# RMS norm with swish on one core: regrouped transfers, two rows by ScalarE in every third unit, and a small scratch transfer ahead of gamma's

## The chip, the cores and the metric

The kernel runs on one core of one Trainium2 chip. Its time is the device time of one execution in microseconds (us), and what stands for a kernel is the median over its runs. A kernel of this size agrees with itself within a few tenths of a microsecond from run to run.

## The reference

The input `x` has 16 x 1024 rows of 512 float32 numbers. Every row is divided by the root of its mean square, scaled by `gamma`, and passed through swish:

```python
rms = np.sqrt(np.mean(x ** 2, axis=-1, keepdims=True) + eps)
x_norm = x / rms * gamma
return (x_norm * (1.0 / (1.0 + np.exp(-x_norm)))).astype(np.float32)
```

33.5 MB are read and 33.5 MB are written; nothing is used twice, so every byte passes the DMA engines once on its way in and once on its way out.

## The kernel before, in words

The 16384 rows are spread over the 128 partitions, so that each partition has 128 rows of 2 KB. The rows of a partition are cut into eleven tiles of 4, 4, 8, six times 16, 8 and 8 rows (`sizes`, L30). A tile is loaded by one DMA and stored by one DMA, from and to the same place in `xb`, a ring of 96 rows a partition (L31, L70). A tile of 16 rows is a transfer of 4 MB. In each partition a tile is one contiguous piece of HBM (L97 to L99), so a transfer consists of 128 packets, one for each partition, of 8, 16 or 32 KB for tiles of 4, 8 or 16 rows.

Loads are issued by SP (L108 to L118), in order. The first two are moved ahead of the program's opening barrier (`early`, L120 to L131). The tiles that begin at rows 96, 112 and 120 use places in the ring that earlier tiles have left: before their loads SP waits for the stores of tiles 0, 1, 2 and of tile 3 (L110 to L117). All other loads are issued at once.

The computation goes in units of four rows (`cn`, L33), 32 of them. For unit k:

- ScalarE (ACT) waits for the tile's load if the unit is the first of its tile (L157, L158). It sums the squares of the fourth row with an accumulating activation (L159), and squares the first three rows into a PSUM buffer, one of two (L166).
- VectorE (DVE) reduces the three squared rows to three sums (`sums`, L204).
- GpSimd (POOL) adds eps (L141) and raises to the power -0.5 (L148).
- VectorE multiplies the four rows by their factor and by gamma, in place, with four instructions (`norm`, L215).
- ScalarE applies silu to the four rows, in place (`swish`, L178).

The order on each engine is written out by hand. VectorE's is sums(k), norm(k-1) (L223 to L233). ScalarE's is square(k), then the stores whose tile has been finished by swish(k-3), then swish(k-2) (L192 to L199). A store is issued from ScalarE's queue (L183) and waits for the count `ends[t]` of finished swishes. So a tile's store stands in ScalarE's instruction order behind the square of a unit three later, and that square may wait for a load. The last tiles' stores come out as soon as their swish is done, because no squares are left then.

Before the loop ScalarE issues the load of gamma, four copies of 2 KB into four partitions of a zeroed tile (L186 to L189), and loads its activation table (L190). VectorE spreads gamma over the partitions with a shuffle (L228) that stands between sums(0) and sums(1), and waits for gamma's landing.

At its end SP waits for the stores (L236 to L238).

Of the kernel before, what the change touches and what calls it, by code (L numbers as in the profile page):

```python
# [8 lines left out]
@with_exitstack  # L9
def kernel(  # L10
    ctx: ExitStack,
    tc: tile.TileContext,
    x: bass.AP,
    gamma: bass.AP,
    eps: bass.AP,
    out: bass.AP,
):
    nc = tc.nc
    P = nc.NUM_PARTITIONS
    AF = mybir.ActivationFunctionType  # L20
    ALU = mybir.AluOpType
    fp32 = mybir.dt.float32
    bf16 = mybir.dt.bfloat16

    xf = x.flatten_outer_dims()
    of = out.flatten_outer_dims()
    R, D = xf.shape


    sizes = [4, 4, 8] + [16] * 6 + [8, 8]  # L30
    ring = 96  # L31
    early = 2
    cn = 4  # L33
    n_sq = 3
    N = sum(sizes)
    assert N * P == R, (N, R)


    tiles = []
    done = 0  # L40
    for sz in sizes:
        assert done % ring + sz <= ring
        tiles.append((done * P, sz, done % ring))
        done += sz
    T = len(tiles)

    chunks = [
        (t, r, r == at)
        for t, (_, sz, at) in enumerate(tiles)
        for r in range(at, at + sz, cn)  # L50
    ]
    K = len(chunks)
    ends = []
    e = 0
    for sz in sizes:
        e += sz // cn
        ends.append(e)

    inv_d = 1.0 / float(D)
    eps_f = float(eps)  # L60

    tc.close()
    tc.compile()  # L65

    def sbuf(name, shape, dt=fp32):
        return nc.alloc_sbuf_tensor(name, shape, dt).ap()

    xb = sbuf("xb", [P, ring, D])  # L70
    gamma4 = sbuf("gamma4", [P, D])
    gamma_sb = sbuf("gamma_sb", [P, D])
    junk = [sbuf(f"junk{i}", [P, D], bf16) for i in range(2)]
    neg_half = sbuf("neg_half", [P, cn])
    ms = sbuf("ms", [P, K, cn])
    aeps = sbuf("aeps", [P, K, cn])
    rstd = sbuf("rstd", [P, K, cn])
    sq = [nc.alloc_psum_tensor(f"sq{i}", [P, 4, D], fp32).ap() for i in range(2)]

    ld = [nc.alloc_semaphore(f"ld{t}") for t in range(T)]  # L80
    st = [nc.alloc_semaphore(f"st{t}") for t in range(T)]
    s_gld = nc.alloc_semaphore("s_gld")
    s_zero = nc.alloc_semaphore("s_zero")
    s_half = nc.alloc_semaphore("s_half")
    s_gamma = nc.alloc_semaphore("s_gamma")
    s_acc = nc.alloc_semaphore("s_acc")
    s_sq = nc.alloc_semaphore("s_sq")
    s_sum = nc.alloc_semaphore("s_sum")
    s_eps = nc.alloc_semaphore("s_eps")
    s_rstd = nc.alloc_semaphore("s_rstd")  # L90
    s_norm = nc.alloc_semaphore("s_norm")
    s_swish = nc.alloc_semaphore("s_swish")

    def need(ins, sem, value):
        return ins.wait_op(sem, value, "sem-ge")

    def dram(ap, t):  # L97
        first, sz, _ = tiles[t]
        return ap[first : first + P * sz].rearrange("(p n) d -> p n d", n=sz)  # L99

    def buf(t):
        _, sz, at = tiles[t]
        return xb[:, at : at + sz, :]


    stored_by_sync = set()

    def load(t):  # L108
        _, sz, at = tiles[t]
        waits = [  # L110
            u for u in range(t)
            if tiles[u][2] < at + sz and at < tiles[u][2] + tiles[u][1]
            and u not in stored_by_sync
        ]
        for u in waits:
            nc.sync.wait_ge(st[u], 16)
            stored_by_sync.add(u)  # L117
        return nc.sync.dma_start(out=buf(t), in_=dram(xf, t)).then_inc(ld[t], 16)  # L118

    entry = nc.main_func.blocks[0].instructions  # L120
    here = nc.cur_bb.bb.instructions
    for t in range(early):
        ins = load(t).ins
        assert here[-1] is ins or here[-1].name == ins.name
        here.pop()
        at = next(
            i for i, other in enumerate(entry)
            if other.engine == mybir.EngineType.SP
            and isinstance(other, mybir.InstDrain)
        )  # L130
        entry.insert(at, ins)  # L131
    for t in range(early, T):
        load(t)


    nc.gpsimd.memset(gamma4, 0.0).then_inc(s_zero, 1)  # L136
    nc.gpsimd.memset(neg_half, -0.5).then_inc(s_half, 1)  # L137
    nc.gpsimd.wait_ge(s_half, 1)
    for k in range(K):
        need(  # L140
            nc.gpsimd.tensor_scalar(  # L141
                out=aeps[:, k, :], in0=ms[:, k, :], scalar1=eps_f, scalar2=None,
                op0=ALU.add,
            ),
            s_sum, k + 1,
        ).then_inc(s_eps, 1)
        need(
            nc.gpsimd.tensor_tensor(  # L148
                out=rstd[:, k, :], in0=aeps[:, k, :], in1=neg_half, op=ALU.pow
            ),  # L150
            s_eps, k + 1,
        ).then_inc(s_rstd, 1)


    def square(k):
        t, at, first = chunks[k]
        if first:  # L157
            nc.scalar.wait_ge(ld[t], 16)  # L158
        acc = nc.scalar.activation(  # L159
            out=junk[k % 2], in_=xb[:, at + n_sq, :], func=AF.Square,  # L160
            scale=inv_d**0.5, accum_out=ms[:, k, n_sq : n_sq + 1],
        )
        if k >= 2:
            need(acc, s_acc, k - 1)
        acc.then_inc(s_acc, 1)
        square = nc.scalar.activation(  # L166
            out=sq[k % 2][:, 0:n_sq, :], in_=xb[:, at : at + n_sq, :],
            func=AF.Square, scale=inv_d**0.5,
        )
        if k >= 2:  # L170
            need(square, s_sum, k - 1)
        square.then_inc(s_sq, 1)

    def swish(k):
        _, at, _ = chunks[k]
        rows = xb[:, at : at + cn, :]
        need(
            nc.scalar.activation(out=rows, in_=rows, func=AF.Silu), s_norm, k + 1  # L178
        ).then_inc(s_swish, 1)

    def store(t):
        need(
            nc.scalar.dma_start(out=dram(of, t), in_=buf(t)), s_swish, ends[t]  # L183
        ).then_inc(st[t], 16)

    need(  # L186
        nc.scalar.dma_start(out=gamma4[0:P:32, :], in_=gamma.partition_broadcast(4)),
        s_zero, 1,
    ).then_inc(s_gld, 16)  # L189
    nc.scalar.preload_act_table_set("silu_and_others")  # L190
    stored = 0
    for k in range(K + 3):  # L192
        if k < K:
            square(k)
        while stored < T and ends[stored] <= k - 2:
            store(stored)
            stored += 1
        if 2 <= k < K + 2:
            swish(k - 2)  # L199


    def sums(k):
        need(
            nc.vector.tensor_reduce(  # L204
                out=ms[:, k, 0:n_sq], in_=sq[k % 2][:, 0:n_sq, :], op=ALU.add,
                axis=mybir.AxisListType.X,
            ),
            s_sq, k + 1,
        ).then_inc(s_sum, 1)

    def norm(k):
        _, at, _ = chunks[k]
        for j in range(cn):
            row = xb[:, at + j, :]
            ins = nc.vector.scalar_tensor_tensor(  # L215
                out=row, in0=row, scalar=rstd[:, k, j : j + 1], in1=gamma_sb,
                op0=ALU.mult, op1=ALU.mult,
            )
            if j == 0:
                need(ins, s_rstd, k + 1)  # L220
        ins.then_inc(s_norm, 1)

    for k in range(K + 1):  # L223
        if k < K:
            sums(k)
        if k == 0:
            need(
                nc.vector.stream_shuffle(gamma_sb, gamma4, [0] * 32), s_gld, 16  # L228
            ).then_inc(s_gamma, 1)
        if k == 1:  # L230
            nc.vector.wait_ge(s_gamma, 1)
        if k >= 1:
            norm(k - 1)  # L233


    for t in range(T):  # L236
        if t not in stored_by_sync:
            nc.sync.wait_ge(st[t], 16)  # L238

# [34 lines left out]
```

## Time and profile before

| | |
|---|---|
| median of 20 runs | 160.31 us (160.13 to 161.45) |
| the profiled execution's own time | 161.45 us |
| its span in the profile | 160.1 us |
| VectorE busy | 139.1 us (87%) |
| ScalarE busy | 125.1 us (78%) |
| HBM read and written | 33.56 MB and 33.55 MB, 419 GB/s over the span |

The span runs from the first to the last thing that the profile shows; the execution's own time has some 1.3 us around it. Times "at" are counted from the span's start. A row of a timeline gives start, duration, engine, line, operation, what it writes and reads, and in brackets how long the engine stood idle before it and what ended that. Besides the instructions, the trace keeps a record of every DMA packet (start, duration, size and queue) and of every semaphore count that a transfer's landing makes; numbers called "packet records" and "landing records" come from there. Queue q1 carries the loads that SP issues, q10 what ScalarE issues.

### The profile page before, as it was taken

To read this page: it belongs to the slowest core of one execution; us is meant where nothing else is said; L and a number is where in the kernel's file an instruction comes from. 1 tells how busy PE (TensorE), PEld (TensorE's weight loads), DVE (VectorE), ACT (ScalarE), POOL (GpSimd) and SP (SyncE) were. 2 spreads that over 40 slices of the span, in tenths; PEclk is the share of its full clock that TensorE was granted. 3 is DMA by queue.
4 is the path that set the end of the run, shared out by engine and by line. 5 is a ranking of instruction groups with operands and counts; after the bars stand their busy time and mean duration, and the time that the engine had idled before them with its cause. 6 is when DMAs were issued, how large, how long until landed. Compare 5 with 4: busy or idle time off the path is not lost.

```text
span 160.1 us, 437 instructions
## 1 busy us (share of the span) xinstructions
DVE 139.1 (87%) x162; ACT 125.1 (78%) x129; POOL 65.4 (41%) x70
## 2 busy tenths in 40 slices
DVE  0299977999999999999999999999999999999100
ACT  1839849888888888998888888888889988874400
POOL 1043552444455555544444444555555444443000
DMA  7999998989999999999999999999999999999993
GB/s 256 442 483 393 393 450 387 473 358 477 475 411 401 417 467 395 450 458 401 434 460 417 393 467 450 405 426 446 426 401 462 389 450 475 434 401 405 438 442 164
DMA packets 3179, 67.14 MB, mean 419 GB/s; under 512 B 356, under 2 KB 356, under 8 KB 360
## 3 DMA queue, kind: packets, MB, share of 16 engines
q1 hardware_dynamic: 1584, 33.56, 49.5%
q10 hardware_dynamic: 1592, 33.56, 48.8%
q14 instruction: 3, 0.02, 0.0%
HBM read 33.56 MB, written 33.55 MB: 419 GB/s over the span
## 4 chain that ended last, share of the span: by engine, by line
DVE 77%; DMA 13%; ACT 2%; issue 0%; SPq 0%; ACTq 0%
DVE xb L215 48%; DVE ms L204 29%; DMA xb<-in_x_dram 13%; ACT xb L178 1%; ACT sq L166 1%; ACT junk L159 0%; SPq L118 0%; ACTq L158 0%
## 5 line engine op out<-in xcount | busy, mean ns | idle before, releaser
L215 DVE SCALAR_TENSOR_TENSOR xb<-xb,rstd,gamma_sb 128x512 f32<-128x512 f32 x128 | 87.2, 743 | 0.0
L178 ACT ACTIVATE xb<-xb 128x2048 f32<-128x2048 f32 x32 | 61.1, 1908 | 16.3 <-DVE xb L215 16.3
L204 DVE TENSOR_REDUCE ms<-sq 128x3 f32<-128x1536 f32 x32 | 56.0, 1750 | 9.5 <-ACT sq L166 9.5
L141 POOL TENSOR_SCALAR aeps<-ms 128x4 f32<-128x4 f32 x32 | 20.7, 646 | 75.7 <-DVE ms L204 75.7
L166 ACT ACTIVATE sq<-xb 128x1536 f32<-128x1536 f32 x32 | 45.9, 1433 | 0.0
L148 POOL TENSOR_TENSOR rstd<-aeps,neg_half 128x4 f32<-128x4 f32 x32 | 44.0, 1376 | 2.7
L159 ACT ACTIVATE junk<-xb 128x512 bf16<-128x512 f32 x32 | 19.7, 615 | 5.5 <-DMA xb<-in_x_dram 5.5
L159 ACT ACTIVATION_READ_ACCUMULATOR junk<-xb 128x1 f32 x32 | 6.0, 186 | 0.0
L190 ACT ACT_TABLE_LOAD x1 | 1.3, 1283 | 3.6 <-issue 3.6
L136 POOL MEMSET gamma<- 128x512 f32 x1 | 0.5, 525 | 1.5 <-POOLq L65 1.5
L228 DVE STREAM_SHUFFLE gamma_sb<-gamma 128x512 f32<-128x512 f32 x1 | 0.7, 719 | 0.0
L255 POOL MEMSET const-float32-0.0<- 128x1 f32 x1 | 0.1, 98 | 0.2 <-issue 0.2
L255 POOL MEMSET const-bfloat16-1.0<- 128x1 bf16 x1 | 0.1, 101 | 0.0
L255 POOL MEMSET const-uint8-127<- 128x1 uint8 x1 | 0.1, 101 | 0.0
L137 POOL MEMSET neg_half<- 128x4 f32 x1 | 0.1, 101 | 0.0
L255 POOL MEMSET const-float32-1.0<- 128x1 f32 x1 | 0.1, 98 | 0.0
L228 DVE LOAD_MASK_SELECT gamma_sb<-gamma x1 | 0.0, 15 | 0.0
## 6 DMA issues: line engine op xcount, KB each, us to landing
xb<-in_x_dram SPq DMA_DIRECT2D x6, 4096.0 KB, 44.6
out_dram<-xb ACTq DMA_DIRECT2D x6, 4096.0 KB, 30.1
xb<-in_x_dram SPq DMA_DIRECT2D x3, 2048.0 KB, 38.6
out_dram<-xb ACTq DMA_DIRECT2D x3, 2048.0 KB, 11.6
xb<-in_x_dram SPq DMA_DIRECT2D x2, 1024.0 KB, 5.9
out_dram<-xb ACTq DMA_DIRECT2D x2, 1024.0 KB, 19.7
gamma<-in_gamma_dram ACTq DMA_DIRECT2D x1, 8.0 KB
```

Source lines behind the costliest of these rows:

```text
L136: nc.gpsimd.memset(gamma4, 0.0).then_inc(s_zero, 1)
L137: nc.gpsimd.memset(neg_half, -0.5).then_inc(s_half, 1)
L141: nc.gpsimd.tensor_scalar(out=aeps[:, k, :], in0=ms[:, k, :], scalar1=eps_f, scalar2=None, op0=ALU.add,),
L148: nc.gpsimd.tensor_tensor(out=rstd[:, k, :], in0=aeps[:, k, :], in1=neg_half, op=ALU.pow),
L159: acc = nc.scalar.activation(out=junk[k % 2], in_=xb[:, at + n_sq, :], func=AF.Square, scale=inv_d**0.5, accum_out=ms[:, k, n_sq : n_sq + 1],)
L166: square = nc.scalar.activation(out=sq[k % 2][:, 0:n_sq, :], in_=xb[:, at : at + n_sq, :], func=AF.Square, scale=inv_d**0.5,)
L178: nc.scalar.activation(out=rows, in_=rows, func=AF.Silu), s_norm, k + 1
L190: nc.scalar.preload_act_table_set("silu_and_others")
L204: nc.vector.tensor_reduce(out=ms[:, k, 0:n_sq], in_=sq[k % 2][:, 0:n_sq, :], op=ALU.add, axis=mybir.AxisListType.X,),
L215: ins = nc.vector.scalar_tensor_tensor(out=row, in0=row, scalar=rstd[:, k, j : j + 1], in1=gamma_sb, op0=ALU.mult, op1=ALU.mult,)
L228: nc.vector.stream_shuffle(gamma_sb, gamma4, [0] * 32), s_gld, 16
L255: nc = _bacc.Bacc("TRN2", target_bir_lowering=False, num_devices=1)
```

## The change

Three things are changed together.

The tiles become groups: two of 8 rows and seven of 16 (`groups`). Loads and stores have lists of their own. The first group is loaded in two pieces of 4 rows and stored as one piece of 8; every other group is loaded and stored whole. So the first two stores of 1 MB are now one of 2 MB, and the two last loads and the two last stores of 2 MB are now one load and one store of 4 MB. The two pieces of the first group are 8 KB of every 16 KB in HBM. The load of the last group waits for the store of group 2, as its two predecessors waited for that of tile 3.

In every third unit (k = 2, 5, 8 ... 29, ten of 32) ScalarE sums the squares of two rows with accumulating activations and squares only two rows into PSUM; VectorE then reduces two rows. The accumulating activations have two semaphores, one for each scratch tile, in place of one.

A transfer of 8 KB, 64 bytes from each of 128 partitions, from a zeroed SBUF tile to a scratch tensor in HBM is issued by ScalarE ahead of gamma's. GpSimd zeroes that tile ahead of gamma's. SP waits for the transfer's landing after it has issued all loads.

```diff
-    sizes = [4, 4, 8] + [16] * 6 + [8, 8]
+    groups = [8, 8] + [16] * 7
     ring = 96
+    loads = [(0, 0, 4), (0, 4, 4), (1, 0, 8)] + [(g, 0, 16) for g in range(2, G)]
+    stores = [(0, 0, 8), (1, 0, 8)] + [(g, 0, 16) for g in range(2, G)]
...
-    n_sq = 3
+    def n_sq(k):
+        return 2 if k % 3 == 2 else 3
...
+    for t in range(early, len(loads)):
+        load(t)
+    nc.sync.wait_ge(s_scratch, 16)
...
+    nc.gpsimd.memset(blank, 0.0).then_inc(s_blank, 1)
     nc.gpsimd.memset(gamma4, 0.0).then_inc(s_zero, 1)
...
+        n = n_sq(k)
+        for j in range(n, cn):
+            acc = nc.scalar.activation(
+                out=junk[j % 2], in_=xb[:, at + j, :], func=AF.Square,
+                scale=inv_d**0.5, accum_out=ms[:, k, j : j + 1],
+            )
+            last = acc_on[j % 2]
+            if last:
+                need(acc, s_acc[j % 2], last)
+            acc.then_inc(s_acc[j % 2], 1)
+            acc_on[j % 2] += 1
         square = nc.scalar.activation(
-            out=sq[k % 2][:, 0:n_sq, :], in_=xb[:, at : at + n_sq, :],
+            out=sq[k % 2][:, 0:n, :], in_=xb[:, at : at + n, :],
...
+    need(nc.scalar.dma_start(out=scratch, in_=blank), s_blank, 1).then_inc(
+        s_scratch, 16
+    )
     need(
         nc.scalar.dma_start(out=gamma4[0:P:32, :], in_=gamma.partition_broadcast(4)),
         s_zero, 1,
...
-                out=ms[:, k, 0:n_sq], in_=sq[k % 2][:, 0:n_sq, :], op=ALU.add,
+                out=ms[:, k, 0 : n_sq(k)], in_=sq[k % 2][:, 0 : n_sq(k), :], op=ALU.add,
```

## The prediction

> **What bounds the kernel now.** I read the page's engine shares first, then its DMA lines, then stages by windows, then the timeline of the end.
>
> ```profile
> DVE 139.1 (87%) x162; ACT 125.1 (78%) x129; POOL 65.4 (41%) x70
> ...
> q1 hardware_dynamic: 1584, 33.56, 49.5%
> q10 hardware_dynamic: 1592, 33.56, 48.8%
> ```
>
> The two queues together hold the 16 DMA engines 98.3% of the span. The windows (the two last numbers are DMA share and GB/s) say that this is no average:
>
> ```profile
> 60.00:100.00 40.00, 40.00 (x46) 35.92 (x37) 18.42 (x18) 1.00 1.00 432
> 100.00:140.00 40.00, 40.00 (x48) 35.92 (x40) 19.27 (x20) 1.00 1.00 432
> ```
>
> VectorE is full in the same stages, so two chains run side by side, and the chain of waits (77% VectorE) names only one. The end shows which is later:
>
> ```profile
> 128.60 1.75 DVE L204 TENSOR_REDUCE ms<-sq 128x3 f32<-128x1536 f32 x1
> 128.71 1.91 ACT L178 ACTIVATE xb<-xb 128x2048 f32<-128x2048 f32 x1 [0.45 <-DVE xb L215]
> 130.27 2.73 DVE L215 SCALAR_TENSOR_TENSOR xb<-xb,rstd,gamma_sb 128x512 f32<-128x512 f32 x4
> ...
> 130.53 0.61 ACT L159 ACTIVATE junk<-xb 128x512 bf16<-128x512 f32 x1
> ...
> 131.14 1.43 ACT L166 ACTIVATE sq<-xb 128x1536 f32<-128x1536 f32 x1
> ...
> 132.91 1.75 DVE L204 TENSOR_REDUCE ms<-sq 128x3 f32<-128x1536 f32 x1
> ...
> 143.60 0.34 ACTq L183 DMA_DIRECT2D out_dram<-xb  x1
> ...
> 150.56 0.34 ACTq L183 DMA_DIRECT2D out_dram<-xb  x1
> ```
>
> The last store goes out at 150.56, but by the packet records its packets start only at 153.1: the stores before it still fill the engines. Compute ends some 2 us before it would hurt, and the DMA engines' work sets the end. Fifteen engines land at 158.0 to 158.6, one lags to 160.1. The median is 160.31, and 1.3 us lie around the span, so a usual run's span is about 159.0; the profiled one (161.45) has a longer lag. I make the sum against 159.0.
>
> **The Trainium skill.** "DMA: Bandwidth & Descriptors", section "Where 436 GB/s comes from", puts the ceiling at 435 GB/s; the stages here run at 432, so it agrees: no faster rate is to be had. The same page, "Queues, rings and completion order", says that an engine alternates between queues packet by packet. The packet records agree: a store packet, a load packet, by turns, whatever their sizes (8 KB 0.309 us, 16 KB 0.611, 32 KB 1.213). "VectorE: DVE Perf Modes", in "The perf-mode tier table", gives `tensor_reduce` one rate only, so its time follows the elements; its shapes here are all 1536 wide, and I price the new one from that.
>
> **Regrouping.** Bytes stay. Per engine, sixteen 8 KB store packets become eight of 16 KB (16 x 0.309 - 8 x 0.611 = 0.06 us), and sixteen 16 KB packets become eight of 32 KB on each side (16 x 0.611 - 8 x 1.213 = 0.07 each): -0.2 us of DMA work.
> What matters is when the last store can start. With the last 16 rows in one store, all else ends when 8 packets of 1.213 are left of the fast engines' stream: 158.0 to 158.6 less 0.35 from packet to landing less 9.7, say 148.1. If the last packets come after that, the engines run dry. In the old kernel half of those 16 rows left at 143.60. Now all leave with the last swish. From issue to packets an idle queue takes 1.0 us at the first engine and 1.6 at the last (the first load: issue at 0.00, packets from 1.01); I take 1.3. Regrouping alone, 150.56 + 1.3 + 9.7 + 0.35 = 161.9: 2.9 us lost.
>
> **Two rows in every third unit.** VectorE's interval is 128.60 to 132.91, 4.31: reduce 1.67, four rows 2.64. The short reduce saves a third of the elements: 1.60 of the 1.67 goes with them (at 1536 elements), so -0.53. ScalarE's loop is the other limit. From a reduce's start: swish starts 0.12 later, takes 1.81 to the next start, accumulation 0.61, squares 1.43, and 0.03 until VectorE starts: 4.00. So after a short unit the next reduce can start 4.00 after, not 3.78: the gain is 4.31 - 4.00 = 0.31 a time, and VectorE waits 0.22. In the short unit itself ScalarE adds one accumulation (0.61) and loses 512 elements of squares (0.43 by the rows of 1536 and 512 elements): 4.18, still under 4.31. Two accumulations back to back are not shown before; between 0.55 and 0.75 each all this stands within 0.1 a time. Of the ten short units k = 5 to 29 lie on the chain, nine: -2.8 us. Unit 2 lies in the opening, where ScalarE waits for loads. POOL's chain (0.66 + 1.39) lies beside and keeps over 1 us of room.
>
> **Scratch transfer.** 128 packets of 64 bytes, 8 per engine. No such packet is in the trace; the 4-byte ones take 9 ns, the 2 KB ones 84. The page's "Specifications" say that under 512 B the engine reads, modifies and writes, so I allow 0.01 to 0.06 us each: +0.1 to +0.5 us of DMA work, taken as +0.15. Cheaper than nothing it can only be if an early write spares the first store something: 32 KB load packets took up to 0.5 us longer at 19 to 21, about 0.5 us an engine, when the first store came in. POOL's extra memset is 0.1 us. ScalarE's extra issue is 0.35 to 1.08 ahead of gamma's and the table load; unit 1 waits 0.54 and unit 2 2.72 us for loads anyway, which hides it. SP's wait stands behind all its load issues and holds nobody.
> Gamma is what can be held. Issued at 2.45 its packets started at 6.4, when the second load was ending; the first store, issued at 16.17, started at 20.2, when the fourth was. ScalarE's requests seem to get in when a load runs out. If scratch takes the place at 6.4, gamma comes at the next, 11.4. The shuffle, behind it sums(1) and norm(0), would then start at 12 instead of 8.63; unit 4 starts at 25.0 to 25.8 instead of 25.03. If scratch gets an earlier place, nothing moves. And with no 1 MB store before the fourth load lands, that comes 0.3 us earlier. Together -0.3 to +0.8; I take +0.3.
>
> **Sum.** Last store 150.56 - 2.8 + 0.3 = 148.05; packets 149.35; end 149.35 + 9.7 + 0.35 = 159.4, with 1.3 around it 160.7. The engines would be dry for 1.2 us, of which the lagging engine's usual 0.6 hides half; the 0.2 less and 0.15 more of DMA work fall into that gap. The two large parts, +2.9 and -2.8, nearly cancel. That is the forecast, 160.7, own range 160.2 to 161.4, chance 0.55 (0.15 of it within 0.2%, which is about what a measurement of this kernel can tell from no change).
>
> **Rival 1: the last load comes late.** Before, unit 28 needed only 8 rows, landed at 118.2; the other 8 landed at 133.5, a little before unit 30 asked for them (134.8). Now all 16 must land before unit 28's squares, at about 124.0 (126.2 less 2.5 saved, plus 0.3). How long they take depends on how many store packets come in between. From 22.0 the engine has 48 load packets (58.2 us). If the first store joins 4 us after its issue at 23, as the old did, four loads are ahead: 44 stores lie between (16 x 0.611 + 28 x 1.213 = 43.7), so 123.9, plus 0.9 of slow packets, 0.35 and 1.3 for the slowest engine: 126.5. ScalarE waits 2.5 and the gain is gone: some 162.9, range 161.5 to 163.2. If instead the store gets in only when that whole load runs out, 8 are ahead, 40 lie between, and it lands at about 121.6, in time. For the second: every later store's first packets stand at a load's end (issued 31.41, started 44.9; 48.67 and 59.4). Chance 0.20, slower.
>
> **Rival 2: the engines never run dry, not slower.** The place is the last store's issue; the point is 146.8, from which its packets arrive by 148.1. VectorE's own pace would give it: 9 x 0.53 = 4.8, so 150.56 - 4.8 = 145.8, if swish did not hold the next squares. Then the DMA work decides, -0.05, and the first store's 0.5 us may go too: 159.0 - 0.05 to 159.0 - 0.55, so 159.8 to 160.3, at 160.0. Against it stands ScalarE's 4.00. Chance 0.25, 0.14 of it faster.
>
> **Numbers.** Faster 0.14; same 0.15 + 0.11 = 0.26; slower 0.40 + 0.20 = 0.60. The range 159.9 to 162.4 leaves out about a tenth below (rival 2's best) and a tenth above (rival 1's upper half).
>
> **What would show it.** Right: VectorE waits about 0.2 us before the reduces that follow a short unit, none before unit 28; the last store is issued near 148; DMA share dips around 148 to 149; its packets last to about 159. Wrong: a ScalarE wait for a load at unit 28 (rival 1); no dip (rival 2); short units that save nothing because two accumulations cost more than 1.3; a shuffle later than 13.

## The result, and the profile after

The changed kernel takes 162.76 us (median), the kernel before 160.3: the ratio is 1.0146 (95% interval 1.0131 to 1.0162), some 2.4 us slower. The forecast was 160.7. Rival 1, the last load that comes late, had 162.9. (Two of the fourteen runs of `e10_first_store_split` and two of the fourteen of `e11_first_and_last_split`, at 163.0 to 165.7 us, are left out of the ratios below as disturbed.)

First the page of the changed kernel: engine shares and queues.

```profile
DVE 134.5 (83%) x162; ACT 126.5 (78%) x149; POOL 65.4 (41%) x71
...
q1 hardware_dynamic: 1440, 33.56, 49.1%
q10 hardware_dynamic: 1448, 33.57, 48.3%
```

VectorE has 4.6 us less to do (the forecast's ten short reduces at 0.53 us would make 5.3), and the span is 1.4 us longer (161.5; the profiled execution of before, 160.1, was a long one). The two queues no longer fill the span: 97.4% against 98.3%. The windows of the changed kernel show where the hole is (the last two columns are again DMA share and GB/s):

```profile
100.00:140.00 40.00, 36.68 (x45) 34.49 (x42) 17.48 (x19) 1.00 1.00 433
140.00:148.00 8.00, 8.00 (x12) 4.55 (x3) 2.99 (x3) 1.00 0.94 406
148.00:151.00 3.00, 0.35 (x1) 1.91 (x1) 0.00 (x0) 1.00 0.00 0
151.00:158.00 7.00, 0.00 (x0) 0.00 (x0) 0.00 (x0) 1.00 1.05 449
```

From 148 to 151 not one packet starts. Before 140 the DMA engines are as full as they were, but there VectorE stands idle for 3.3 of the 40 us, where it had no idle time before. The timeline of the changed kernel says what it waits for:

```profile
107.20 0.63 ACT L176 ACTIVATE junk<-xb 128x512 bf16<-128x512 f32 x1 [0.48 <-DMA xb<-in_x_dram]
...
109.30 1.76 DVE L227 TENSOR_REDUCE ms<-sq 128x3 f32<-128x1536 f32 x1 [0.74 <-ACT sq L185]
...
117.94 1.22 DVE L227 TENSOR_REDUCE ms<-sq 128x2 f32<-128x1024 f32 x1
...
121.95 1.76 DVE L227 TENSOR_REDUCE ms<-sq 128x3 f32<-128x1536 f32 x1
...
126.55 0.63 ACT L176 ACTIVATE junk<-xb 128x512 bf16<-128x512 f32 x1 [2.79 <-DMA xb<-in_x_dram]
...
128.64 1.76 DVE L227 TENSOR_REDUCE ms<-sq 128x3 f32<-128x1536 f32 x1 [2.29 <-ACT sq L185]
...
150.32 0.34 ACTq L202 DMA_DIRECT2D out_dram<-xb  x1
```

The row at 109.30 is unit 24, the rows at 121.95 and 128.64 are units 27 and 28. The kernel before had, for unit 27:

```profile
124.28 1.75 DVE L204 TENSOR_REDUCE ms<-sq 128x3 f32<-128x1536 f32 x1
```

So unit 27 is 2.3 us ahead of the kernel before. Unit 28 starts at 128.64, where it was at 128.60: all of it is gone. ScalarE waited 2.79 us for the last group's load, and the last store goes out at 150.32 as against 150.56. By the packet records its packets start at 151.16, and the engines had nothing from 149.0 on, most of them from 148.2. The landing record of that load has its last engine at 126.46. In the chain of waits it is one long piece, reached from the end:

```profile
76.67 49.79 DMA xb<-in_x_dram
126.46 0.02 issue
```

So the loss stands in two places that need each other: the load holds compute back to its old pace, and the last store, now one of 4 MB, finds the engines dry.

### The profile page after: what moved, and what is told of

Same layout as the page of the kernel before. It is cut to its first block, busy times and chain, and to the rows that moved or that the text cites. A ratio compares the mean times of both kernels' runs of the same rounds, so it can differ in the third digit from the quotient of the medians.

```text
span 161.5 us, 455 instructions
## 1 busy us (share of the span) xinstructions
DVE 134.5 (83%) x162; ACT 126.5 (78%) x149; POOL 65.4 (41%) x71
## 4 chain that ended last, share of the span: by engine, by line
DMA 54%; DVE 23%; ACT 13%; issue 1%; POOL 0%; ACTq 0%; POOLq 0%
DMA xb<-in_x_dram 31%; DMA out_dram<-xb 18%; DVE xb L238 15%; DVE ms L227 7%; ACT xb L197 7%; DMA gamma<-in_gamma_dram 5%; ACT sq L185 4%; ACT junk L176 2%; DVE gamma_sb L251 0%; POOL gamma L149 0%; POOL blank L148 0%; ACTq L173 0%; POOLq L67 0%
## 5 line engine op out<-in xcount | busy, mean ns | idle before, releaser
L227 DVE TENSOR_REDUCE ms<-sq 128x3 f32<-128x1536 f32 (+1 forms) x32 | 50.8, 1586 | 11.5 <-ACT sq L185 10.2
L185 ACT ACTIVATE sq<-xb 128x1536 f32<-128x1536 f32 (+1 forms) x32 | 41.6, 1299 | 0.0
L176 ACT ACTIVATE junk<-xb 128x512 bf16<-128x512 f32 x42 | 25.8, 615 | 7.1 <-DMA xb<-in_x_dram 6.9
L176 ACT ACTIVATION_READ_ACCUMULATOR junk<-xb 128x1 f32 x42 | 7.8, 186 | 0.0
```

The costliest lines, as they stand in the source:

```text
L176: acc = nc.scalar.activation(out=junk[j % 2], in_=xb[:, at + j, :], func=AF.Square, scale=inv_d**0.5, accum_out=ms[:, k, j : j + 1],)
L185: square = nc.scalar.activation(out=sq[k % 2][:, 0:n, :], in_=xb[:, at : at + n, :], func=AF.Square, scale=inv_d**0.5,)
L227: nc.vector.tensor_reduce(out=ms[:, k, 0 : n_sq(k)], in_=sq[k % 2][:, 0 : n_sq(k), :], op=ALU.add, axis=mybir.AxisListType.X,),
```

## The experiments

**The theory (late load).** SP's queue and ScalarE's take turns on every DMA engine, a packet each, whatever their sizes. The moment at which the first store comes in settles how many load packets get ahead of the stores, and the size of the store packets in between settles how long the rest of the loads take. The first store now comes in later, which helps the loads, but two stores of small packets have become one of packets twice as large, and a store of 32 KB packets has moved up between the loads, which costs them more: the last group lands near 126.5, after unit 28 asks for it. **Rivals:** the scratch transfer costs, itself or through gamma; the two rows gain nothing or cost; the last store's size alone is what is lost; the last load is late for another reason (its semaphore, the ring).

### Each of the three changes alone

`e1_no_scratch` takes the scratch transfer out of the changed kernel:

```diff
-    nc.sync.wait_ge(s_scratch, 16)
...
-    nc.gpsimd.memset(blank, 0.0).then_inc(s_blank, 1)
...
-    need(nc.scalar.dma_start(out=scratch, in_=blank), s_blank, 1).then_inc(
-        s_scratch, 16
-    )
```

> The changed kernel without the scratch transfer, its memset and SP's wait for it. Late-load theory (the last group's load lands near 126.5 and holds unit 28, and the last store finds the engines dry): the scratch transfer is hidden, gamma lands near 7.5 instead of 11.2 and nothing behind it moves; 162.7 us, between 162.4 and 162.9, ScalarE's wait for a load at unit 28 still 2.8 us. Rival, the scratch transfer itself costs (0.1 to 0.5 us of engine time, or through gamma's late landing): 162.2 us or less.

Measured: 162.67 us, ratio to before 1.0141 (1.0112 to 1.0169). The wait at unit 28 is 2.83 us, the last store goes out at 150.34. Gamma's packets start at 6.5 instead of 9.0, and it helps nothing. The scratch transfer is not the cause.

`e8_scratch_only` is the kernel before with that transfer. It and the next kernel are made from the changed file, with the old tiles put back:

```diff
+    nc.sync.wait_ge(s_scratch, 16)
...
+    nc.gpsimd.memset(blank, 0.0).then_inc(s_blank, 1)
...
+    need(nc.scalar.dma_start(out=scratch, in_=blank), s_blank, 1).then_inc(
+        s_scratch, 16
+    )
```

> The kernel before with the scratch transfer alone. Late-load theory: 128 packets of 11 ns are 0.09 us an engine, gamma's late landing is hidden by the waits for the third and fourth load: 160.4 us, between 160.1 and 160.7. Rival, an early write spares the first store something, or costs more than its packets: below 160.0 or above 160.8.

Measured: 160.21 us, ratio 0.9994 (0.9975 to 1.0012). No difference that can be told.

`e2_two_rows_only` is the kernel before with the two rows:

```diff
-    n_sq = 3
+    def n_sq(k):
+        return 2 if k % 3 == 2 else 3
```

> The kernel before with the two rows in every third unit alone (tiles as before, no scratch transfer). Late-load theory: the last store is issued some 2.5 us earlier than 150.56, its packets queue behind the others, and the DMA engines end where they ended: 160.3 us, between 160.0 and 160.6. Rival, the extra accumulations cost ScalarE more than they spare VectorE: over 161.

Measured: 160.43 us, ratio 1.0002 (0.9985 to 1.0020). Its last store goes out at 148.05, 2.5 us earlier than before, and its packets start at 152.95, behind the others. A compute that ends 2.5 us earlier is worth nothing here, where the DMA engines still have a backlog.

`e3_groups_only` is the changed kernel with three rows everywhere and no scratch transfer (besides the lines below, those of `e1_no_scratch` are gone):

```diff
-        return 2 if k % 3 == 2 else 3
+        return 3
```

> The changed kernel with three rows in all units and no scratch transfer, so the groups alone. Late-load theory: unit 28 asks for its rows near 126, they land near 126.5, so there is almost no wait left, and the last store goes out near 150.8 as against 150.3 in the changed kernel: 163.2 us, between 162.8 and 163.6. The two rows are then worth 0.5 us in the changed kernel, not 2.8. Rival, the two rows keep their 2.8 us beside the groups: 165.5.

Measured: 163.07 us, ratio 1.0169 (1.0135 to 1.0203). Unit 28 waits 0.99 us for a load that again lands at 126.43; the last store goes out at 150.58. The groups make the whole loss, and behind the late load the two rows win back only 0.4 us (163.07 here, 162.67 in `e1_no_scratch`).

### The last group's store and load

`e5_last_store_split` stores the last group in halves:

```diff
-    stores = [(0, 0, 8), (1, 0, 8)] + [(g, 0, 16) for g in range(2, G)]
+    stores = [(0, 0, 8), (1, 0, 8)] + [(g, 0, 16) for g in range(2, G - 1)]
+    stores += [(G - 1, 0, 8), (G - 1, 8, 8)]
```

> The changed kernel with the last group's store in two halves of 8 rows; loads as changed. Late-load theory: the load wait at unit 28 stays 2.8 us, the first half is issued near 143.4 and its packets cover 148.2 to 153.1, the second half is issued near 150.3 and finds the engines busy: 160.2 us, between 159.8 and 160.6. Rival, the late compute costs in itself: about 162.7.

Measured: 160.37 us, ratio 1.0003 (0.9994 to 1.0012). ScalarE's wait at unit 28 is as it was, 2.81 us, the halves are issued at 143.11 and 150.07. Its windows, for the stretch in which the changed kernel's engines stood still:

```profile
140.00:148.00 8.00, 8.00 (x11) 4.30 (x3) 2.75 (x3) 1.00 0.95 412
148.00:151.00 3.00, 0.10 (x1) 1.91 (x1) 0.00 (x0) 1.00 1.00 426
```

The first half fills the hole, and the whole 2.4 us come back although compute stays late. One half of the cause is shown.

`e4_last_load_split` loads the last group in halves, with the store whole:

```diff
-    loads = [(0, 0, 4), (0, 4, 4), (1, 0, 8)] + [(g, 0, 16) for g in range(2, G)]
+    loads = [(0, 0, 4), (0, 4, 4), (1, 0, 8)] + [(g, 0, 16) for g in range(2, G - 1)]
+    loads += [(G - 1, 0, 8), (G - 1, 8, 8)]
```

> The changed kernel with the last group's load in two halves of 8 rows, one semaphore each; stores as changed. Late-load theory in its packet form (each load packet lets one 32 KB store packet through, so halves of 8 packets each pay for 8 store packets): the first half lands near 122 and unit 28 doesn't wait, the second lands near 136, later than the whole did, and unit 30, which asks near 132, waits about 4 us; last store near 151.7, 164.0 us, between 163.3 and 164.6. Rival, it was only that one semaphore covered all 16 rows: both halves in time, last store near 148, 160.7 us.

Measured: 164.26 us, ratio 1.0248 (1.0230 to 1.0265). The first half lands at 122.02 and unit 28 doesn't wait; the second lands at 136.90, ten us after the whole load of the changed kernel. ScalarE's waits of this run (total, times, longest):

```profile
ACT junk L177 <- DMA xb<-in_x_dram: 8.6, 6, 4.0
```

The longest, 4.0, stands before unit 30; the last store goes out at 152.41. What looks like a finer, kinder load is slower, because a half has as many packets as a whole (8 an engine), and each of them lets one 32 KB store packet through. The packet records bear the count out: from the first store's entry to the end of the loads the changed kernel has 44 load packets left an engine and 44 store packets come between them; here it is 52 and 52. The semaphore was not the point.

### The first store

`e7_first_store_later` issues the first store two units later; `e9_first_store_one_later` has `+ (stored == 0)` in its place, one unit:

```diff
-        while stored < len(stores) and ends[stored] <= k - 2:
+        while stored < len(stores) and ends[stored] + 2 * (stored == 0) <= k - 2:
```

> The changed kernel with the first store issued two units later, together with the second (near 31 instead of 22.4); nothing else moves. Late-load theory: 7 more load packets go ahead of the stores, so the last group lands 7 x 1.21 = 8.5 us earlier, near 118, the waits at units 24 and 28 (0.5 and 2.8 us) vanish, the last store goes out near 147.4, and the engines are dry for less than 0.5 us: 160.4 us, between 160.0 and 160.8. Rival, the last group's landing is set by something else (the ring, or the store that its load waits for): 162.7 us as changed.

Measured: 163.59 us, ratio 1.0205 (1.0143 to 1.0268), outside the range. The load went as expected: issued at 29.36, packets in at 33.10 instead of 26.39, the last group on average over the engines at 118.65 instead of 125.37 (6.7 later in, 6.7 earlier out; the last engine at 122.34), no wait at units 24 and 28, the last store at 147.74. The time did not. In the profiled execution, the fastest of the four with 162.41, thirteen engines landed the last store at 158.68 to 158.84, the others at 159.56, 159.90 and 161.05 (so three lag, and not one behind fifteen, as the next expectation has it). At 83 already one landing of a load is late (83.25 against a mean of 79.4); the records don't name the engine.

This run also answers the rival of the ring. Here the last load was issued at 84.08 and in the changed kernel at 76.67, since it waits for a store to free its place; issued 7.4 us later it landed earlier.

> The changed kernel with the first store issued one unit later (near 26.5 instead of 22.4). Late-load theory: its packets come in near 30.5, 3.4 load packets more go ahead, the last group lands 4.1 us earlier, near 122.3, before unit 28 asks (123.6); no wait at units 24 and 28, last store near 147.4. If all engines keep step the time is 160.4 us, 160.0 to 160.8. Rival, formed on the run with the first store two units later (its waits vanished and its last store went out at 147.74, yet one DMA engine landed 2.0 us after the other fifteen): load packets that run far ahead of the stores themselves make an engine lag; then 162 or more here too.

Measured: 160.63 us, ratio 1.0024 (1.0008 to 1.0039). The store was issued at 24.77, not 26.5, so the shift is smaller: in at 28.76, the last group at 124.15, 2.3 us earlier for 2.4 later; ScalarE waits 0.95 us at unit 28 and the last store goes out at 148.01. No engine fell far behind in the profiled execution. The numbers are those of the forecast (last store 148.05, 160.7 us), but with a load wait that the forecast did not have.

`e10_first_store_split` stores the first group in its two old pieces:

```diff
-    stores = [(0, 0, 8), (1, 0, 8)] + [(g, 0, 16) for g in range(2, G)]
+    stores = [(0, 0, 4), (0, 4, 4), (1, 0, 8)] + [(g, 0, 16) for g in range(2, G)]
```

> The changed kernel with the first group's store in two pieces of 4 rows, as the tiles before had them; loads, last store, two rows and scratch transfer as changed. Late-load theory in its packet form: engines take turns packet by packet, so between the loads lie still 44 to 48 store packets, but eight more of them are of 0.31 us and eight fewer of 1.21; the last group lands 3.5 to 4.5 us earlier, near 122 to 123, unit 28 waits 0 to 0.5 us, last store near 147.6: 160.6 us, between 160.2 and 161.0. Rival, an earlier first store takes its share from the loads, so that the last group lands later than 126.5: 163 or more.

Measured: 160.44 us, ratio 1.0005 (0.9985 to 1.0025). The last group lands at 121.72, although the first store came in at 21.78 instead of 26.39. The timeline of ScalarE in this run, at the same unit as above:

```profile
121.44 1.89 ACT L197 ACTIVATE xb<-xb 128x2048 f32<-128x2048 f32 x1
123.23 0.61 ACT L176 ACTIVATE junk<-xb 128x512 bf16<-128x512 f32 x1
...
147.51 0.34 ACTq L202 DMA_DIRECT2D out_dram<-xb  x1
```

Unit 28 starts at 123.23 without a wait (no bracket), and the last store goes out 2.8 us earlier than in the changed kernel. Its first packets are there at 148.35. The other changes all stand, the 4 MB load and the 4 MB store too: one line about the kernel's first store undoes the whole loss. The second half of the cause is shown.

`e11_first_and_last_split` adds the last store's halves to it:

```diff
+    stores = [(0, 0, 4), (0, 4, 4), (1, 0, 8)] + [(g, 0, 16) for g in range(2, G - 1)]
+    stores += [(G - 1, 0, 8), (G - 1, 8, 8)]
```

> The same with the last group's store in two halves besides. Late-load theory: the engines never run dry, DMA work decides, 160.2 us, between 159.9 and 160.5, so the last store's size is worth at most 0.5 us once the load is in time, as against 2.4 us in the changed kernel. Rival, the last store's size is worth its 2 us whatever the load does: 2 us below the run beside it.

Measured: 160.46 us, ratio 1.0000 (0.9989 to 1.0012). With the load in time the last store's size is worth nothing that can be told from 160.44.

`e13_first_split_three_rows` is `e10_first_store_split` with three rows in all units (`return 3` in `n_sq`):

> The changed kernel with the first group's store in two pieces and three rows in all units, so without the two rows; the last group's load is in time (near 122). Theory: the last store goes out near 150.4 (unit 4 starts as before), its packets begin 0.85 us later, the engines are dry from 148.2 to 151.2, and the last packets land near 161.3: 162.6 us, between 162.2 and 162.9, so the two rows are worth 2.1 us here (160.44 with them), four times what they are worth behind the late load (0.4). Rival, the two rows are worth as little here as there: 161 or less.

Measured: 163.57 us, ratio 1.0205 (1.0159 to 1.0250), outside the range. The chain of the profiled execution is as expected: last store at 150.59, packets from 151.44, last landing 161.70; its own time is 163.06. Two of the other three were at 164.1 and 164.2; why is open, no trace shows those. With the load in time the two rows are worth 2.5 us of span (161.7 less 159.2 in the profiled executions), behind the late load 0.4 of time.

### One engine that lags

`e12_later_and_last_split` joins two edits from above, to see whether the miss of `e7_first_store_later` was a dry stretch:

> The changed kernel with the first store two units later and the last store in two halves. If the time of the run with the first store two units later (163.59) came from the engines running dry: 160.3 us. If it came from one DMA engine that lags behind the others, which no later work can hide: 162 to 164 again, with one landing of the last store 2 us or more after the others.

```diff
-    stores = [(0, 0, 8), (1, 0, 8)] + [(g, 0, 16) for g in range(2, G)]
+    stores = [(0, 0, 8), (1, 0, 8)] + [(g, 0, 16) for g in range(2, G - 1)]
+    stores += [(G - 1, 0, 8), (G - 1, 8, 8)]
...
-        while stored < len(stores) and ends[stored] <= k - 2:
+        while stored < len(stores) and ends[stored] + 2 * (stored == 0) <= k - 2:
```

Measured: 164.54 us, ratio 1.0256 (1.0231 to 1.0280). In its windows the tail is not a hole but a few engines still at work:

```profile
150.00:158.00 8.00, 0.00 (x0) 0.00 (x0) 0.00 (x0) 1.00 0.97 416
158.00:161.00 3.00, 0.00 (x0) 0.00 (x0) 0.00 (x0) 1.00 0.27 115
161.00:163.10 2.10, 0.00 (x0) 0.00 (x0) 0.00 (x0) 1.00 0.07 31
```

The last store's landings run from 157.74 to 163.10, and the spread was there at 104 (a load with a mean of 99.94 and its last engine at 104.70). So the miss of `e7_first_store_later` was a lag of one or a few DMA engines and not a dry stretch. Between 70 and 106 single packets took some hundred ns more than the same size takes elsewhere. In the profiled executions of both kernels with the first store two units later a load's last engine came 4.2 and 6.1 us behind the median engine; in no other profiled execution was it more than 2.9. Unprofiled runs of other kernels with an early last load are long too (four of twenty of `e9_first_store_one_later` at 161.5 to 161.8, one of `e10_first_store_split` at 162.13, while the kernel before had at most 161.35 beside them); whether that is the same lag isn't shown. Why an engine lags is open: no run here varies it alone.

### The main runs side by side

From issue records, packet records and landing records, in us from the span's start:

| kernel | first store issued, first packet | load that unit 28 needs, last engine | wait at unit 28 | last store issued | time |
|---|---|---|---|---|---|
| before | 16.17, 20.18 | 118.15 | 0 | 150.56 | 160.3 |
| changed | 22.36, 26.39 | 126.46 | 2.79 | 150.32 | 162.76 |
| groups alone | 22.23, 26.50 | 126.43 | 0.99 | 150.58 | 163.07 |
| last load in halves | 22.64, 26.58 | 122.02 | 0 (4.0 at unit 30) | 152.41 | 164.26 |
| last store in halves | 22.19, 26.64 | 126.22 | 2.81 | 150.07 | 160.37 |
| first store one unit later | 24.77, 28.76 | 124.15 | 0.95 | 148.01 | 160.63 |
| first store in halves | 18.25, 21.78 | 121.72 | 0 | 147.51 | 160.44 |
| the same, three rows | 18.50, 22.07 | 121.97 | 0 | 150.59 | 163.57 |
| first store two units later | 29.36, 33.10 | 122.34 | 0 | 147.74 | 163.59 |

No version beats the kernel before by more than a measurement can tell: where the DMA engines neither run dry nor lag, the 67 MB at 432 GB/s set the time. The last row is slow by a lag, the other slow ones by engines that run dry.

## Why the prediction was wrong

**The step that failed** is when the first store gets in, the choice inside rival 1: "If instead the store gets in only when that whole load runs out, 8 are ahead, 40 lie between, and it lands at about 121.6, in time. For the second: every later store's first packets stand at a load's end (issued 31.41, started 44.9; 48.67 and 59.4)." The forecast rests on that second case, so its sum has no term for a load wait. What happened was the first, with four loads ahead: the store was issued at 22.36, its packets came in at 26.39, 44 store packets lay between the loads, and the last load landed at 126.46, not 121.6. ScalarE waited 2.79 us for it, and of the 2.8 us that the sum gives the two rows 0.4 was left (`e3_groups_only` less `e1_no_scratch`).

The text had the number for it: 16.17 to 20.2 and 2.45 to 6.4, twice 4.0 us. I read both as "at a load's end", because that is where they fell. The runs here put the first store's delay at 3.5 to 4.5 us from issue to first packet in every kernel, wherever the load stood; what sets these 4 us no run shows. The later stores begin when the store ahead of them in their own queue runs out. In the kernel before that is a load's end, since the first came in at one (32 load packets an engine started by then, and each load has 8) and a store takes 8 turns: the next three came in at about 40, 48 and 56. In the changed kernel the first came in at 36 and the next three at 44, 52 and 60, each in the middle of a load. So the load's end was a coincidence of when the old first store came in. The Trainium skill's sentence on taking turns ("DMA: Bandwidth & Descriptors", "Queues, rings and completion order") agrees with these counts (44 load and 44 store packets an engine in the changed kernel after the first store's entry); I had cited it and then drawn the entry of the store from something else.

Rival 1's own numbers were right: landing 126.5 (126.46), a wait of 2.5 us (2.79), 162.9 us (162.76). The range was built wrongly beside it: it ended at 162.4, below that rival's value, so that by its own account the larger part of the rival's 0.20 lay outside and not the tenth that the text said.

**Regrouping** was right in size: 161.9 of span for the groups alone, and 161.7 in `e3_groups_only`. That run has a load wait of 0.99 us that the sum did not have, made up by its earlier start; `e13_first_split_three_rows`, without the wait, has 161.7 too. The 1.3 us from the last store's issue to its packets were 0.84. The same page's "Latency and other measured facts" has 0.6 us for the first byte of such a queue. The runs show more, and they decide: 0.84 to 0.85 for the last store with empty engines, 1.01 for the first load, and some 4 us for the first store with loads queued, which the page doesn't tell apart.

**The two rows** were right where no load held them: after a short unit the next reduce starts 4.01 us later (117.94 to 121.95; 4.00 forecast), the short reduce takes 1.22 against 1.75, two accumulations in a row 0.61 each. The last store came 2.5 us earlier in `e2_two_rows_only` (2.8 forecast). That VectorE's own pace would give more (rival 2) is refuted by the same 4.01.

**The scratch transfer** was right in its small effect and off in detail: its packets took 11 ns (0.09 us an engine; 0.15 taken). Gamma was held, but for less than I feared: its packets came at 9.04 to 10.12, not 11.4, the shuffle at 11.24. Unit 4 started at 24.49, 0.5 us earlier than before, where +0.3 was taken: the fourth load landed 0.7 us earlier (22.20 against 22.86), and no store lay in front of it.

**The dip** was forecast for 148 to 149 and lay from 148.2 to 151.16: the 1.2 us of the sum, plus 2.3 that VectorE waited at unit 28 and 0.7 at unit 24 (a load again), less 0.8 for the earlier start and 0.5 for the shorter entry, make 2.9 of the 3.0 us.

## What to carry to other kernels

Where two queues take turns on the DMA engines by packet, as here, count packets, not bytes: what a load waits for is the number of packets in front and the size of those that come in between, so splitting a store early can bring a load late in the kernel forward, and splitting a load can push it back. Take the moment at which a store gets in from the delay after its issue, not from where the other queue stands. Before a transfer is merged, ask for each consumer when its whole piece lands, since the merged piece has the landing of its last row. And when a gain in one place is to pay for a loss in another, both must hold at once: here the 2.5 us of compute that the two rows save alone were cancelled by a load wait of 2.8, and either half of the cause, put right alone, gave all of it back.

## What the runs showed of the hardware that was not expected

The first store from ScalarE's queue started its packets 3.5 to 4.5 us after issue while SP's loads were queued (fourteen kernels), and the last store 0.84 to 0.85 us after issue when the engines were empty. Moving the first store's entry by 2.4 and 6.7 us (`e9_first_store_one_later`, `e7_first_store_later`) moved a load a hundred us later by 2.1 and 6.7 us (means of the engines), almost one for one. 64-byte packets to HBM took 11 ns each. Single DMA engines landed the last store 2.3 us (`e7_first_store_later`) and 4.8 us (`e12_later_and_last_split`) behind the median engine, and such a lag sets the end as surely as late compute does.
